# Splitting the mixer and output weights once, ahead of their units, and loading the halves from DRAM

## The chip, the cores and the metric

One core of a Trainium2 chip runs the kernel. The metric is the device time of one execution in microseconds (us); lower is better. TensorE (PE) multiplies, VectorE (DVE), ScalarE (ACT) and GpSimd (POOL) work elementwise, and SyncE (SP) issues every DMA of this kernel, in order, from one queue. Each engine, too, executes its instructions in the order in which they stand.

## The reference

One streaming step of an encoder layer, for 32 + 1024 = 1056 tokens of 1024 features, in float32. Cut to what matters:

```python
x = x + 0.5 * rmsnorm(swiglu(rmsnorm(x), w_gate1, w_up1, w_down1))   # first feed-forward part
h = rmsnorm(x)
p = h @ w_in                              # 1024 x 3072: conv value and gate, and q, k, v, g of 4 heads
c = silu(layernorm(causal_conv31(a * sigmoid(b))))
r = silu(g) * groupnorm(retention(rope(q), rope(k), v))
x = x + rmsnorm(concat(c, r) @ w_out)     # 1024 x 1024
x = x + 0.5 * rmsnorm(swiglu(rmsnorm(x), w_gate2, w_up2, w_down2))   # second feed-forward part
```

The hidden width of a feed-forward part is 2816. The 32 sample tokens carry a state in; all new states are outputs.

## The kernel before

**Splits.** A float32 operand is split into two parts that TensorE multiplies fast: `hi`, a copy rounded to fp32r, and `lo`, the rest, so that a product is hi·hi + hi·lo + lo·hi, three matmuls (L276, L324). For a weight tile `split` (L144) lets ScalarE copy the raw tile to `whi` (L147) and GpSimd, or for some pieces VectorE, subtract to `wlo` (L148). Activations are split by ScalarE and VectorE (L238, L248, L574).

**Units.** The work is a list of units, written out in order by `unit` (L354) and run by `run` (L360). A unit is a block of weights with 512 columns of contraction or less, and one or two visits, each for one half `j` of the tokens (528 of them, as 2 x 264). A visit of a "plain" unit (`visit_plain`, L268) makes four output blocks, 96 matmuls in all where the contraction is 4 x 128; the other kinds, "seven" and "packed", use seven products in place of eight (`visit`, L307). `prep` (L157) is a generator for each unit: it fetches the raw tiles (L155), and then splits them piece by piece. `run` calls it between the products of the unit before (`between`, `plan`), and lets the raw tiles of unit n + 2 be fetched when unit n is done. Raw tiles have 5 buffers, `wh` and `wl` 7 each.

**Order.** The author's code keeps a clock of its own (`now`, advanced by `MM_US` for each matmul) and places work that isn't matmuls at times on it (`later`, `at`); a scheduler then orders each engine's instructions by priority and its own estimate of time. `load` (L113) ties a DMA's place to the matmul that was last written.

**Stages.** First the gate and up units of the first feed-forward part: for each of 11 pairs `fp_` of hidden blocks a gate and an up unit (`up_unit`, L549). The hidden activations are split and spilled to DRAM (`spill`, L567: tiles `hh` and `hl`, tag "g", two buffers; DRAM tensors `hth` and `htl`). Then the down units (L659), in five blocks `DBLK` of 1, 2, 2, 2 and 4 hidden pairs: the spilled tiles come back as `tah`, `tal`, `tbh`, `tbl` (`load_t`, L629), asked for a block ahead by `build` (L642). Norms follow (`post_norm`, `pre_norm`).

The mixer (L701) has 24 plain units: for each half, 4 convolution units (`cu`, L1025) and 4 heads with two units each (`hu`, L1028). Its weights `win` have 12 blocks, each used by both halves, and each time fetched and split anew. VectorE works off the convolution's 31 taps per tile one after the other between other work (`tap`, L757; L760 and L762, 8 tiles). The retention (`retain`, L876) goes in three steps per chunk of tokens: TensorE, ScalarE and VectorE (L884 to L892), then TensorE, VectorE, a power on GpSimd (L927), VectorE (L929), then TensorE and VectorE (L934, L936). The output projection has 8 plain units (L977), from 4 blocks of `wo`, each again fetched and split for either half. The second feed-forward part is as the first.

Of the kernel before, what the change touches and what calls it, by code (L numbers as in the profile page):

```python
# [15 lines left out]
P = 128  # L16
# [39 lines left out]
SPILL_STEP = (1.4, 2.8, 5.6, 9.0)  # L56
POST_STEP = 3.0
NEXT_DELAY = (16.0, 3.0)
MM_US = 0.124
# [6 lines left out]
def layer_kernel(ctx: ExitStack, tc: tile.TileContext, a: dict, o: dict):  # L66
# [90 lines left out]
    def prep(src, nk, kind, dve_lo):  # L157
# [51 lines left out]

        return ws, {"seven": seven, "packed": packed, "plain": plain}[kind]()  # L210

# [148 lines left out]
    def run(opening):  # L360
# [8 lines left out]
        for n, (src, nk, visits, _, kind) in enumerate(program):  # L369
            ws = made[n][0]  # L370
            nxt = made[n + 1][1]
            each = 4 if kind.startswith("plain") else 7
            total = each * len(visits)
            if n + 1 < len(program):
                nkind = program[n + 1][4]
                pieces_ = {"seven": 7, "packed": (7 * program[n + 1][1] + 3) // 4, "plain": 4}[nkind]

                if nkind == kind == "seven":
                    plan = [max(0, total - 8 - (total > 7) * 3)] + [total - 7 + i for i in range(7)]
                else:  # L380
                    plan = [0] + [total - 1 - (pieces_ - 1 - i) * max(1, min(2, (total - 1) // pieces_)) for i in range(pieces_)]
            else:
                plan = []
# [10 lines left out]
            for before, tj, dst, acc, after in visits:  # L394
                if before:
                    before()
                if kind == "plain":
                    visit_plain(ws, tj, nk, dst, after, between, acc)
# [145 lines left out]
    def ffn(xt, wgu, wdn, res, gpost, out, gpre, nxt, lead, first):  # L544
# [4 lines left out]
        def up_unit(fp_, j):  # L549
            def gate_dst():  # L550
                f = hb[fp_, j] = ftile("h")
                return [f[:, i] for i in (0, 3, 1, 2)]
# [106 lines left out]
        for b, (k0, nk) in enumerate(DBLK):  # L659
# [23 lines left out]
            def start(b=b, nk=nk):  # L683
                if b == 0:
                    alloc()
                if b + 1 < len(DBLK):
                    us = 21 * nk * MM_US
# [265 lines left out]
    def out_proj(wt, res, gpost, out, gpre, nxt, also):  # L953
# [23 lines left out]
        for j in (0, 1):  # L977
            for m in range(4):
                unit(a["wo"][m], 4, [o_visit(m, j)], kind="plain")

# [30 lines left out]
    def begin(j):  # L1011
# [4 lines left out]
        for i, b in enumerate(bs):  # L1016
            nrm.add(b, 0.0 if j == 0 else 2.0 * i, sq[i // 2][:, 4 * (i % 2):4 * (i % 2) + 4] if j == 0 else None)
        pre_norm(j, bs, nrm, "f1pre", xt[0], first[0] if j == 0 else None, False, (0.0, 0.0) if j == 0 else (10.0, 3.0),
                 (lambda: later(BEGIN_DELAY, lambda: begin(1))) if j == 0 else lambda: None)

    ffn(xt[0], a["wgu1"], a["wd1"], a["x"], "f1post", x1, "mpre", xt[1], 3, first[0])
    conv, head, free = mixer(xt[1], xt[2])
    win = a["win"]

    def cu(i, j):  # L1025
        unit(win[i], 4, [conv(i, j)], kind="plain")

    def hu(h, j):  # L1028
        for i, v in enumerate(head(h, j)):
            unit(win[4 + 2 * h + i], 4, [v], kind="plain")  # L1030

# [79 lines left out]
```

## Time and profile before

| | us |
|---|---|
| median of 3 runs | 2088.27 (2088.16 to 2093.26) |
| the profiled execution, own time | 2090.26 |
| its span, first to last instruction | 2088.4 |
| TensorE busy | 1931.3 (92%) |
| VectorE busy | 1431.8 (69%) |
| ScalarE busy | 824.4 (39%) |
| GpSimd busy | 1003.0 (48%) |
| mean granted TensorE clock | 0.978 of full speed |

Stages in the profiled execution, by when their instructions begin: gate and up units to 512 us, down units to 783, mixer to 1200, output projection to 1305, then the second feed-forward part.

How to read the profile: every row is of one profiled execution. A group's row has the line of the kernel, the engine and operation, output<-input by the program's names, the shapes, the count; then the busy time, the mean of one in ns, and the idle time of the engine just before, with what ended it. A wait "A <- B" has the total, the number of times, and the longest. `PEclk` is the TensorE clock that was granted, and the DMA share is the mean busy share of the 16 DMA engines. Busy time of TensorE is not TensorE at its peak, so its count in a stretch is set beside it.

### The profile page before, as it was taken

What the parts mean: (1) busy time and instruction counts of PE and PEld (TensorE: products, weight loads), DVE (VectorE), ACT (ScalarE), POOL (GpSimd) and SP (SyncE); (2) the same over time, 40 slices, a digit from 0 to 9 for tenths busy, and PEclk for the clock granted to TensorE, in tenths of its full rate; (3) what the DMA queues carried; (4) which work ended last, traced back from release to release, by engine and by line L of the source; (5) the groups of instructions that cost most, each with busy time, mean ns of one, the idle gap of its engine ahead of it and who ended that gap; (6) DMA issues with size and microseconds to landing.
All of it is one profiled execution on the core that took longest, in us unless ns stands there. A gap on an engine that the chain in (4) does not pass through costs nothing. (4 is left out here: it accounts for less than half of the span.)

```text
span 2088.4 us, 39191 instructions
## 1 busy us (share of the span) xinstructions
PE 1931.3 (92%) x15272; PEld 1889.8 (90%) x15272; DVE 1431.8 (69%) x2386; ACT 824.4 (39%) x1550; POOL 1003.0 (48%) x718
## 2 busy tenths in 40 slices
PE   5988999999999998899889998998999999999995
PEld 4988999999899998888879898987999999989995
DVE  6777666544677368999999846988676644477545
ACT  5444444444322234333343355444444444422221
POOL 3756444454254454455444445456554445344441
PEclk9999999999999999999989999999999999999998
DMA  4354334333965653223422353425344323676742
GB/s 156 98 187 154 129 118 154 132 103 137 351 223 168 216 161 121 62 77 90 125 77 74 106 194 116 148 78 176 115 165 156 129 92 125 240 262 224 254 137 83
DMA packets 143977, 308.60 MB, mean 148 GB/s; under 512 B 17456, under 2 KB 47536, under 8 KB 143792
## 3 DMA queue, kind: packets, MB, share of 16 engines
q1 hardware_dynamic: 143792, 306.10, 44.3%
q8 instruction: 120, 1.97, 0.4%
q14 instruction: 65, 0.53, 0.1%
HBM read 217.54 MB, written 88.50 MB: 147 GB/s over the span
## 5 line engine op out<-in xcount | busy, mean ns | idle before, releaser
L148 POOL TENSOR_TENSOR wlo<-raw,whi 128x512 fp32r<-128x512 f32 x604 | 875.4, 1465 | 847.8 <-ACT whi L147 686.0
L147 ACT ACTIVATE whi<-raw 128x512 fp32r<-128x512 f32 x616 | 363.5, 617 | 647.7 <-issue 172.7
L325 PE MATMUL px<-tbh,whi 128*128 128x264 f32 x832 | 238.6, 287 | 4.3 <-DVE ys L313 2.4
L762 DVE SCALAR_TENSOR_TENSOR cu<-cu,vec 128x558 f32<-128x558 f32 (+1 forms) x240 | 239.6, 1017 | 1.0
L277 PE MATMUL px<-tbh,whi 128*128 128x264 f32 x768 | 226.4, 295 | 11.3 <-ACT cu L727 6.1
L325 PE MATMUL px<-tbh,wlo 128*128 128x264 f32 x832 | 236.6, 284 | 0.0
L325 PE MATMUL px<-tbl,whi 128*128 128x264 f32 x832 | 236.3, 284 | 0.0
L277 PE MATMUL px<-tbl,whi 128*128 128x264 f32 x768 | 223.7, 291 | 0.6 <-DVE tbl L249 0.6
L277 PE MATMUL px<-tbh,wlo 128*128 128x264 f32 x768 | 222.4, 290 | 0.0
L325 PEld LDWEIGHTS px<-tbh,whi 128*128 128x128 f32 x832 | 156.9, 189 | 6.6 <-ACT h L315 2.8
L277 PEld LDWEIGHTS px<-tbh,whi 128*128 128x128 f32 x768 | 149.3, 194 | 12.3 <-ACT cu L727 6.3
L325 PEld LDWEIGHTS px<-tbl,whi 128*128 128x128 f32 x832 | 156.8, 188 | 0.0
L325 PEld LDWEIGHTS px<-tbh,wlo 128*128 128x128 f32 x832 | 156.7, 188 | 0.0
L277 PEld LDWEIGHTS px<-tbl,whi 128*128 128x128 f32 x768 | 148.6, 194 | 1.2 <-DVE tbl L249 0.9
L277 PEld LDWEIGHTS px<-tbh,wlo 128*128 128x128 f32 x768 | 148.5, 193 | 0.2 <-issue 0.2
L318 DVE TENSOR_TENSOR h<-h,px 128x264 f32<-128x264 f32 x152 | 59.0, 424 | 113.3 <-PE px L325 106.1
L325 PE MATMUL px<-tah,whi 128*128 128x264 f32 x416 | 121.0, 291 | 12.0 <-ACT whi L147 8.0
L325 PE MATMUL py<-tbh,whi 128*128 128x264 f32 x416 | 121.7, 293 | 11.0 <-DVE h L318 9.1
L325 PE MATMUL pz<-tbh,whi 128*128 128x264 f32 x416 | 121.5, 292 | 5.2 <-DVE h L318 2.2
L325 PE MATMUL pz<-tah,wlo 128*128 128x264 f32 x416 | 119.6, 287 | 4.9 <-DVE wlo L148 3.1
L325 PE MATMUL py<-tah,whi 128*128 128x264 f32 x416 | 121.1, 291 | 3.2 <-DVE h L601 1.7
L325 PE MATMUL pz<-tbl,whi 128*128 128x264 f32 x416 | 119.4, 287 | 4.5 <-DVE tbl L239 4.5
(218 smaller groups left out, 6030.6 us busy)
## 6 DMA issues: line engine op xcount, KB each, us to landing
raw<-in_wgu SPq DMA_DIRECT2D x224, 256.0 KB, 3.3
hth<-hh SPq DMA_DIRECT2D x28, 924.0 KB, 4.0
htl<-hl SPq DMA_DIRECT2D x28, 924.0 KB, 4.9
raw<-in_win SPq DMA_DIRECT2D x96, 256.0 KB, 3.3
tbh<-hth SPq DMA_DIRECT2D x44, 528.0 KB, 5.8
tbl<-htl SPq DMA_DIRECT2D x44, 528.0 KB, 6.1
raw<-in_wd SPq DMA_DIRECT2D x64, 256.0 KB, 3.0
raw<-in_wd SPq DMA_DIRECT2D x96, 128.0 KB, 3.5
```

The source lines that it names most:

```text
L147: nc.scalar.activation(hi, x[:, :n], AF.Copy)
L148: (nc.vector if dve else nc.gpsimd).tensor_tensor(lo, x[:, :n], hi, ALU.subtract)
L277: mm = nc.tensor.matmul(ps, l[:, w], r, start=k == 0 and i == 0 and n == 0, stop=k == nk - 1 and i == 1 and n == 2)
L318: nc.vector.tensor_tensor(to, to, ps, ALU.add)
L325: mm = nc.tensor.matmul(ps, l[:, w], r, start=start and k == 0 and i == 0, stop=k == nk - 1 and i == 2, skip_group_check=True)
L762: nc.vector.scalar_tensor_tensor(cc, u[:, t:t + m], vec[:, w + t:w + t + 1], cc, ALU.mult, ALU.add)
```

## The change

The 16 weight blocks of mixer and output projection (12 of `win`, 4 of `wo`) are split once, during the first feed-forward part, and kept in DRAM as `hi` and `lo` (tensors `wm`). A block is made in two pairs of its four 128x512 tiles, 32 pairs in all. A pair (`make_pair`) takes one tile of tag "g" (`mk`), loads two raw tiles into one half of it (2 x 256 KB), copies them to the other half on ScalarE (128x1024), subtracts on GpSimd (128x1024), and stores `hi` and `lo` (512 KB each). Eight pairs are placed in the gate and up units, two at each gate unit of the last four `fp_`; the other 24 in the down units, ten of them 12 us apart on the author's clock, then 14 of them 7.5 us apart.

The units of mixer and output projection are of a new kind, "made": `ready_made` loads the four `hi` and four `lo` tiles of a unit straight into `wh` and `wl` buffers (three of each) and two `raw` buffers, and splits nothing. `visit_plain` is unchanged. Their fetches stay where they were: for unit n + 2 when unit n is done.

```diff
+MAKE_STEP = (4.5, 9.0)
...
+        def ready_made():
+            for p in range(4):
+                tags = ("wh", "wl") if p < 3 else ("raw", "raw")
+                pair = []
+                for x, t in zip(src, tags):
+                    w = wp.tile([P, 4 * P], F32R, name=nm("w" + t), tag=t, **({"bufs": 5} if t == "raw" else {}))
+                    load(w.bitcast(F32), x[:, p])
+                    pair.append(w)
+                ws.append(tuple(pair))
+            yield
...
+    def make_later(name, src):
+
+        made_w[name] = hi, lo = [drm.tile([P, 4, 4 * P], F32, name=nm("wm")) for _ in range(2)]
+        to_make.extend((src, hi, lo, q) for q in (0, 1))
+
+    def make_weights(dt):
+        if to_make:
+            later(dt, lambda x=to_make.pop(0): make_pair(*x))
+
+    def make_pair(src, hi, lo, q):
+        n = 4 * P
+        g = flat(fp.tile([P, 8, Q], F32R, name=nm("mk"), tag="g", bufs=2))
+        x, h = g[:, 0:2 * n], g[:, 2 * n:4 * n]
+        for i, b in enumerate(((0, 3), (1, 2))[q]):
+            load(x[:, i * n:(i + 1) * n].bitcast(F32).rearrange("p (k c) -> p k c", k=4), src[:, b])
+
+        def split2():
+            nc.scalar.activation(h, x.bitcast(F32), AF.Copy)
+            nc.gpsimd.tensor_tensor(x, x.bitcast(F32), h, ALU.subtract)
+
+        def store():
+            for to, v in ((hi, h), (lo, x)):
+                nc.sync.dma_start(out=to[:, 2 * q:2 * q + 2], in_=v.bitcast(F32).rearrange("p (a c) -> p a c", a=2))
+
+        later(MAKE_STEP[0], split2)
+        later(MAKE_STEP[1], store)
...
             def gate_dst():
+                if fp_ >= DBLK[-1][0] and j == 0:
+                    for dt in (0.5, 2.5):
+                        make_weights(dt)
...
                 if b == 0:
                     alloc()
+                    for i in range(len(to_make)):
+                        make_weights(12.0 + 12.0 * i if i < 10 else 132.0 + 7.5 * (i - 10))
...
-                unit(a["wo"][m], 4, [o_visit(m, j)], kind="plain")
+                unit(made_w["wo", m], 4, [o_visit(m, j)], kind="made")
...
-        unit(win[i], 4, [conv(i, j)], kind="plain")
+        unit(made_w["win", i], 4, [conv(i, j)], kind="made")
...
-            unit(win[4 + 2 * h + i], 4, [v], kind="plain")
+            unit(made_w["win", 4 + 2 * h + i], 4, [v], kind="made")
```

The new lines move those below: L147 to L148, L148 to L149, L155 to L156, L114 to L115, L927 to L973.

The order of GpSimd in the mixer, second and third convolution tile (`cu`) of the first half and the first head's retention, before; `wlo` are weight halves, `rs` the retention's powers, `tl` the tail of a convolution tile:

```order
L719 MEMSET cu_9809 128x30
L742 COPY tl_10010<-cu_9809 128x30
L927 TENSOR_TENSOR rs_9782<-rs_9782,mhalf 32x1
L927 TENSOR_TENSOR rs_9884<-rs_9884,mhalf 124x1
L148 TENSOR_TENSOR wlo_10210<-raw_10015,whi_10209 128x512
L148 TENSOR_TENSOR wlo_10260<-raw_10220,whi_10259 128x512
L148 TENSOR_TENSOR wlo_10293<-raw_10221,whi_10292 128x512
L148 TENSOR_TENSOR wlo_10331<-raw_10222,whi_10330 128x512
L927 TENSOR_TENSOR rs_9961<-rs_9961,mhalf 124x1
L927 TENSOR_TENSOR rs_10069<-rs_10069,mhalf 124x1
L148 TENSOR_TENSOR wlo_10364<-raw_10223,whi_10363 128x512
L148 TENSOR_TENSOR wlo_10408<-raw_10368,whi_10407 128x512
```

And the same place of GpSimd after the change:

```order
L765 MEMSET cu_10041 128x30
L788 COPY tl_10226<-cu_10041 128x30
L973 TENSOR_TENSOR rs_10010<-rs_10010,mhalf 32x1
L973 TENSOR_TENSOR rs_10112<-rs_10112,mhalf 124x1
L973 TENSOR_TENSOR rs_10185<-rs_10185,mhalf 124x1
L973 TENSOR_TENSOR rs_10293<-rs_10293,mhalf 124x1
L973 TENSOR_TENSOR rs_10367<-rs_10367,mhalf 124x1
L765 MEMSET cu_10584 128x30
```

The splits between the powers are gone, and the powers follow each other.

The order of SP in the second block of the down units, after the change: `raw` from `in_wd` are the block's weights, four tiles to a unit, `tah` to `tbl` spilled tiles, `mk` a make's loads, `wm` its stores:

```order
L156 DMA raw_6440<-in_wd 128x256
L115 DMA mk_6281<-in_win 128x512 x2
L115 DMA tah_6284<-hth_120 128x792
L115 DMA tbh_6286<-hth_120 128x1056
L115 DMA tbl_6287<-htl_121 128x1056
L156 DMA raw_6443<-in_wd 128x256
L115 DMA tah_6461<-hth_120 128x792
L156 DMA raw_6442<-in_wd 128x256
L115 DMA tal_6462<-htl_121 128x792
L156 DMA raw_6441<-in_wd 128x256
L115 DMA mk_6494<-in_win 128x512 x2
L248 DMA wm_96<-mk_6281 128x1024
```

Before, the same place held the weights and spilled tiles alone; now about two loads and two stores of a pair stand among each unit's four weight tiles.

The order of GpSimd at the same place, after the change:

```order
L149 TENSOR_TENSOR wlo_6435<-raw_6347,whi_6434 128x256
L244 TENSOR_TENSOR mk_6281<-mk_6281 128x1024
L149 TENSOR_TENSOR wlo_6527<-raw_6440,whi_6526 128x512
L149 TENSOR_TENSOR wlo_6552<-raw_6441,whi_6551 128x512
L149 TENSOR_TENSOR wlo_6573<-raw_6442,whi_6572 128x512
L149 TENSOR_TENSOR wlo_6592<-raw_6443,whi_6591 128x256
L244 TENSOR_TENSOR mk_6494<-mk_6494 128x1024
```

Here a make's subtraction has come between the last split of one unit and the first of the next; ScalarE's copies stand in the same way.

More of the change, by code (lines that the diff above doesn't have):

```diff
@@ L208, in plain @@
                 yield
-        return ws, {"seven": seven, "packed": packed, "plain": plain}[kind]()
+        def ready_made():
[8 more added lines that the diff above has]
+            yield
+        return ws, {"seven": seven, "packed": packed, "plain": plain, "made": ready_made}[kind]()
+    made_w, to_make = {}, []
+    def make_later(name, src):
[18 more added lines that the diff above has]
+        later(MAKE_STEP[1], store)
     PART = ((0, 0), (1, 0), (0, 1), (1, 1), (0, 2), (1, 3), (1, 2))
@@ L371, in run @@
             nxt = made[n + 1][1]
-            each = 4 if kind.startswith("plain") else 7
+            each = 4 if kind in ("plain", "made") else 7
             total = each * len(visits)
@@ L375, in run @@
                 nkind = program[n + 1][4]
-                pieces_ = {"seven": 7, "packed": (7 * program[n + 1][1] + 3) // 4, "plain": 4}[nkind]
+                pieces_ = {"seven": 7, "packed": (7 * program[n + 1][1] + 3) // 4, "plain": 4, "made": 1}[nkind]
                 if nkind == kind == "seven":
@@ L396, in run @@
                     before()
-                if kind == "plain":
+                if kind in ("plain", "made"):
                     visit_plain(ws, tj, nk, dst, after, between, acc)
@@ L1019, in begin @@
                  (lambda: later(BEGIN_DELAY, lambda: begin(1))) if j == 0 else lambda: None)
+    win = a["win"]
+    for m in range(4):
+        make_later(("wo", m), a["wo"][m])
+    for x in "h0 c0 c1 h1 c2 h2 c3 h3".split():
+        i = int(x[1])
+        for u in (i,) if x[0] == "c" else (4 + 2 * i, 5 + 2 * i):
+            make_later(("win", u), win[u])
     ffn(xt[0], a["wgu1"], a["wd1"], a["x"], "f1post", x1, "mpre", xt[1], 3, first[0])
     conv, head, free = mixer(xt[1], xt[2])
-    win = a["win"]
     def cu(i, j):
-        unit(win[i], 4, [conv(i, j)], kind="plain")
+        unit(made_w["win", i], 4, [conv(i, j)], kind="made")
     def hu(h, j):
         for i, v in enumerate(head(h, j)):
-            unit(win[4 + 2 * h + i], 4, [v], kind="plain")
+            unit(made_w["win", 4 + 2 * h + i], 4, [v], kind="made")
     for j in (0, 1):
```

## The prediction

> **What bounds the kernel now.** I read the page's busy times first, then the busy times by stage, then who waits for whom in the mixer, and last the queue of the DMAs.
>
> ```profile
> PE 1931.3 (92%) x15272; PEld 1889.8 (90%) x15272; DVE 1431.8 (69%) x2386; ACT 824.4 (39%) x1550; POOL 1003.0 (48%) x718
> ```
>
> TensorE is busy 92% of the whole, so the question is where the rest is lost. The stages, with each engine's busy time, its count, then the granted clock, the DMA share and GB/s (the first row is the end of the first feed-forward part's gate and up units, three are its down units, three the mixer, the last the output projection):
>
> ```profile
> core 0: us, PE busy (x) PEld busy (x) DVE busy (x) ACT busy (x) POOL busy (x), PEclk, DMA share, GB/s
> 365.00:512.00 147.00, 146.50 (x1203) 146.08 (x1203) 67.79 (x112) 64.77 (x122) 70.92 (x51) 1.00 0.33 111
> 512.00:574.00 62.00, 58.55 (x449) 55.68 (x448) 39.12 (x90) 23.41 (x55) 19.37 (x16) 1.00 0.97 346
> 574.00:678.00 104.00, 100.95 (x791) 99.60 (x792) 75.90 (x190) 24.71 (x43) 50.77 (x43) 0.97 0.60 195
> 678.00:783.00 105.00, 103.28 (x857) 102.86 (x856) 52.47 (x81) 32.39 (x49) 50.47 (x36) 1.00 0.57 189
> 783.00:835.00 52.00, 45.38 (x359) 44.25 (x358) 42.16 (x53) 25.39 (x44) 23.05 (x17) 0.93 0.40 121
> 835.00:1148.00 313.00, 275.65 (x2107) 265.86 (x2106) 301.29 (x512) 116.59 (x245) 150.87 (x113) 0.95 0.29 85
> 1148.00:1200.00 52.00, 47.42 (x377) 46.66 (x376) 44.13 (x90) 19.30 (x45) 26.73 (x21) 0.97 0.35 103
> 1200.00:1305.00 105.00, 99.70 (x836) 99.07 (x834) 60.85 (x100) 55.66 (x104) 51.83 (x39) 0.99 0.49 155
> ```
>
> The first row is TensorE at full rate: 147.00 us / 1203 = 122 ns a matmul. By that price the mixer's 359 + 2107 + 377 = 2843 matmuls need 347 us, and they take 417: 70 us are lost there, some of it as a clock of 0.93 to 0.97. In the long middle stretch VectorE is busy 301.29 of 313.00 us, 96%. That is the limit there, and TensorE's waits name it:
>
> ```profile
> PE uo L906 <- DVE on L929: 10.7, 7, 6.8
> PE rp L934 <- DVE on L929: 5.9, 4, 3.6
> PE px L277 <- ACT cu L727: 6.1, 1, 6.1
> PE px L277 <- DVE ys L670: 4.8, 1, 4.8
> PE uo L909 <- DMA st<-in_sret: 3.9, 2, 2.3
> ```
>
> VectorE is so full because of GpSimd. Groups from 745 to 1310 us (mixer and output units, with a few splits of the down part), with the count, the busy time and the mean in ns:
>
> ```profile
> L148 POOL TENSOR_TENSOR wlo<-raw,whi 128x512 fp32r<-128x512 f32 x142 | 221.6, 1580 | 144.6 <-ACT whi L147 139.1 <-DMA cu<-in_sconv 2.5 <-PE px L277 1.1
> L147 ACT ACTIVATE whi<-raw 128x512 fp32r<-128x512 f32 x140 | 80.7, 623 | 115.1 <-issue 44.6 <-PE py L277 32.0 <-PE pz L277 31.4
> L762 DVE SCALAR_TENSOR_TENSOR cu<-cu,vec 128x558 f32<-128x558 f32 x120 | 121.7, 1031 | 0.7
> L762 DVE SCALAR_TENSOR_TENSOR cu<-cu,vec 128x528 f32<-128x528 f32 x120 | 118.0, 1002 | 0.3
> ```
>
> VectorE, and below it GpSimd, in order of time (start, length, count at the end):
>
> ```profile
> 900.96 2.91 DVE L762 SCALAR_TENSOR_TENSOR cu<-cu,vec 128x558 f32<-128x558 f32 x4
> 913.22 0.78 DVE L762 SCALAR_TENSOR_TENSOR cu<-cu,vec 128x558 f32<-128x558 f32 x1
> 915.65 2.54 DVE L762 SCALAR_TENSOR_TENSOR cu<-cu,vec 128x558 f32<-128x558 f32 x2
> ```
>
> ```profile
> 902.41 0.12 POOL L719 MEMSET cu<- 128x30 f32 x1 [6.91 <-DMA rd<-hd]
> 912.26 4.62 POOL L148 TENSOR_TENSOR wlo<-raw,whi 128x512 fp32r<-128x512 f32 x2 [1.34 <-ACT whi L147]
> ```
>
> GpSimd stood idle for 6.91 us before 902.41, and there four convolution taps took 2.91 us, 0.73 each. Under the split at 912.26 two took 2.54, 1.27 each. So the splits of the mixer's weights pay twice: their own time on GpSimd, off the path, and the taps' longer time on VectorE, on it.
>
> **The change, part by part.**
>
> *Splits leave the mixer.* Before, 24 units there and 8 of the output projection each split four tiles: 128 copies on ScalarE (623 ns) and 128 subtractions on GpSimd (1580 ns, 202 us). None is left. The 240 taps take 121.7 + 118.0 = 240 us; at 0.73 they take 175, at 0.78 they take 187: VectorE gets 53 to 65 us back, about 52 of them in the middle stretch. What is late next: VectorE then has 301 - 52 = 249 us of work there and TensorE 2107 x 0.122 = 258. Two queues that wait for each other do not both run full; in the stretches before and behind, VectorE is busy 81% (42.16 of 52) and 85%. With 88% in the middle I get 249 / 0.88 = 283 us, 30 less than now. The edges (TensorE needs 44 and 46 us of their 52) I give 2 and 4. Mixer: -36 us. Ends: -12, if the retention's round trips between TensorE and VectorE are what costs and not the load; -60, near TensorE's floor of -70. Output projection: 836 x 0.122 = 102 of 105 us, so -1.
>
> *Direct loads in the mixer.* A unit now loads eight tiles of 256 KB in place of four. That is 1.05 MB more per 11.7 us (96 matmuls), 90 GB/s on top of 85 to 121. The second stretch of the table, at 346 GB/s, shows room for twice that. The loads wait on the SP queue for TensorE to let go of the tiles of the unit before the last one, no longer for GpSimd, which now costs SP this much in the mixer:
>
> ```profile
> SPq L155 <- POOL wlo L148: 234.2, 79, 14.2
> SPq L938 <- DVE hd L936: 20.8, 6, 6.8
> ```
>
> Stores that wait for VectorE (the second row, 3.5 us each) stand in the same queue, ahead of some loads; a load has a unit's time to land, so I take nothing, and up to +10 inside the ends above.
>
> *Makes in the gate and up units.* Eight pairs, each two loads, a copy and a subtraction of 128x1024, and two stores of 512 KB. The copy is about 1.05 us by the row of nearest size, the subtraction about 2.8, twice the row of 512:
>
> ```profile
> L248 ACT ACTIVATE tbh<-ys 128x1056 fp32r<-128x1056 f32 x8 | 8.7, 1085 | 6.2 <-DVE ys L480 6.1
> L148 POOL TENSOR_TENSOR wlo<-raw,whi 128x512 fp32r<-128x512 f32 x77 | 104.7, 1373 | 111.3 <-ACT whi L147 100.8 <-PE py L325 6.4 <-DMA xs<-in_x 3.3
> ```
>
> From 365 to 512 us GpSimd is busy 70.92 of 147, ScalarE 64.77 and the DMA share is 0.33, which hides 23 us, 8 us and 12.6 MB. The pairs use the two buffers of the spills (hh, hl), so a spill can wait for a store. +1, ends 0 and +6.
>
> *Makes in the down units.* 24 pairs. GpSimd gets 67 us more (77 splits take 104.7 of 271 us now) and ScalarE 25; on both, in the new order, a make stands between the last split of one unit and the first of the next, where GpSimd waits for loads today. A make's copy waits for its load, and the next unit's splits stand behind it; but their weights were asked for after that load. A make's store waits for GpSimd's subtraction, and the next weight loads stand behind it on SP; but these wait for splits that stand behind the same subtraction. So the queues add little. By the taps' loss, 0.54 us for each 1.58 us of split, 67 us more of GpSimd would cost VectorE 23 us; but most of its work there reads PSUM, and that is no slower beside a busy GpSimd:
>
> ```profile
> L318 DVE TENSOR_TENSOR ys<-ys,px 128x264 f32<-128x264 f32 x41 | 17.3, 426 | 3.8 <-PE px L325 2.9
> ```
>
> The stage's VectorE time is 167 of 271 us besides, so I take nothing. The Trainium skill ("SBUF — State Buffer", Who interferes with whom) has a rule that speaks for nothing as well: only VectorE operations with two SBUF inputs contend with a GpSimd operation that reads SBUF, and the loser blocks fully. By that rule the two-input operations of the norms at the stage's end would wait up to 2.8 us for each make that they meet; the trace has no make, and I leave it in the ends.
>
> The DMAs are the real price. A pair moves 1.57 MB, all 24 move 37.7 MB; the three down rows moved 346 x 62 + 195 x 104 + 189 x 105 = 61.6 MB. Together 99.3 MB in 271 us, 366 GB/s. What the queue can do (a stretch of 10 us), how long tiles took to land from 505 to 640 us (the last number), and GpSimd's splits for the second block:
>
> ```profile
> 540.00:550.00 10.00, 9.06 (x71) 8.61 (x70) 6.05 (x17) 5.86 (x15) 0.03 (x1) 1.00 1.03 401
> ```
>
> ```profile
> raw<-in_wd SPq DMA_DIRECT2D x40, 128.0 KB, 3.8
> tbl<-htl SPq DMA_DIRECT2D x14, 528.0 KB, 6.7
> ```
>
> ```profile
> 549.97 2.84 POOL L148 TENSOR_TENSOR wlo<-raw,whi 128x512 fp32r<-128x512 f32 x2 [12.23 <-ACT whi L147]
> 562.30 4.86 POOL L148 TENSOR_TENSOR wlo<-raw,whi 128x512 fp32r<-128x512 f32 x4 [6.43 <-ACT whi L147]
> 575.56 4.69 POOL L148 TENSOR_TENSOR wlo<-raw,whi 128x512 fp32r<-128x512 f32 x4 [8.40 <-ACT whi L147]
> ```
>
> Full, it moves 357 GB/s (346 / 0.97) to 401: the stage needs 248 to 278 us of DMA for its 271. The Trainium skill ("DMA: Bandwidth & Descriptors", Specifications) gives about 358 GB/s per core as the limit of the memory; by that the stage would need 277 us and be bound by it, but the row of 401 lies above that limit. While the share is 0.97 a unit's splits begin 12.3 and 13.3 us apart (549.97, 562.30, 575.56), though TensorE needs 84 x 0.122 = 10.3: raw tile, load, additions, split and release follow each other. A pair's 1.57 MB per unit adds 0 to 4.2 us to that cycle, for four units 0 to 17; I take 8. Behind 580 us the share falls to 0.6 and TensorE is busy 97%; I take 2 us each for blocks three and four and for the last block. Down part: +12, ends 0 and +51 (below).
>
> **Sum.** -36 - 1 + 1 + 12 = -24 us. The profiled execution took 2090.26 us (span 2088.4), 2.0 above the median of the runs, 2088.27, so I forecast 2088.3 - 24 = 2064 us.
>
> **The rivals.**
> *The copies' traffic is hidden and VectorE's relief goes through whole*: mixer -52 (the taps at 0.78), output -2, +1, +2: -51, 2037 us. For it: 401 GB/s. Against: TensorE's small waits in the mixer have many releasers.
> *The down part becomes bound by DMA*, and the kernel slower. At 12 us a pair brings 131 GB/s, so from 574 to 678 the share is 0.60 + 0.37 = 0.97, as in the second block: eight units at 12.8 us in place of 10.3, +20. The second block itself gets all 17. In the last block a pair comes every 7.5 us, 210 GB/s: 0.57 + 0.59 = 1.16 of its 105 us, +14 at 401 GB/s or so. +51 in all, against -36: 2088 + 15 = 2103 us. It decides if weight tiles of the down part land in 8 us, not 3.8, behind 580 us, for then the chain has no reserve. Against it: tiles from hth and htl are asked for a block ahead, and pairs can drift into the mixer with its share of 0.29.
> *The splits move and nothing else does*: the mixer's loss is the retention's round trips (TensorE waits for L929, not for taps): -12 there, +12 in the down part: 2088 us.
>
> **Chances.** Forecast 0.64, hidden traffic 0.14, no change 0.10, bound by DMA 0.12. About 0.3%, 6 us, can be told from no change. So faster 0.78, same 0.10, slower 0.12. The range goes from 2036 (the hidden case) to 2090 (mixer at its low end), and leaves out the DMA-bound case and the tails, 2 in 10.
>
> **What would show it.** Right: taps at 0.73 to 0.78 us with both shapes near 770 ns on the mean; VectorE under 90% in the mixer's middle; the mixer some 36 us shorter at a clock nearer 1.00; the DMA share of 574 to 783 us at 0.9 or more, and the down part 5 to 20 us longer, most of it in the second block, with TensorE waiting there for wlo, whi or raw. Wrong: taps still at 1.0 us; a mixer as long as now beside a VectorE that idles; a down part longer by over 35 us, or not at all.

## The result, and the profile after

The changed kernel takes 2068.51 us (median of 5 runs, 2064.78 to 2076.89), the kernel before, on the same chip, 2089.7 (2088.16 to 2093.26): a ratio of 0.99 (95% interval 0.9883 to 0.9917), 21 us less. The forecast was 2064 (2036 to 2090). The sum agrees better than its terms do, so the stages are gone through one by one.

The profiled execution of the changed kernel is the slowest of its five, 2076.89 us, 8.4 above their median; against the 2090.26 of before it is 13.4 us shorter, and that is what its stages can add up to. Busy times and the DMAs' total, from the page of after:

```profile
PE 1929.3 (93%) x15272; PEld 1888.5 (91%) x15272; DVE 1384.3 (67%) x2386; ACT 785.5 (38%) x1454; POOL 892.1 (43%) x622
...
DMA packets 180843, 392.51 MB, mean 189 GB/s; under 512 B 21553, under 2 KB 51633, under 8 KB 180657
```

TensorE has the same 15272 matmuls. GpSimd lost 96 instructions net (128 subtractions gone, 32 of double size come), and the DMAs carry 84 MB more.

Busy times by stage of after (columns as in the prediction's table: busy time and count of each engine, granted clock, DMA share, GB/s). The bounds are, to 1 or 2 us, where the same matmul, counted from the first, begins as at the bounds of before:

```profile
core 0: us, PE busy (x) PEld busy (x) DVE busy (x) ACT busy (x) POOL busy (x), PEclk, DMA share, GB/s
365.00:531.00 166.00, 153.78 (x1207) 151.88 (x1206) 80.33 (x109) 70.17 (x130) 91.51 (x59) 0.97 0.51 173
531.00:597.00 66.00, 60.35 (x450) 57.19 (x448) 41.50 (x98) 26.16 (x58) 25.39 (x19) 0.97 1.00 360
597.00:713.00 116.00, 103.89 (x795) 99.69 (x796) 84.74 (x188) 32.58 (x51) 71.02 (x52) 0.99 0.88 298
713.00:823.00 110.00, 106.27 (x852) 105.45 (x851) 55.75 (x80) 40.20 (x54) 65.13 (x41) 0.97 0.93 328
823.00:874.00 51.00, 44.89 (x361) 43.90 (x360) 40.72 (x55) 20.92 (x33) 15.25 (x8) 0.93 0.92 295
874.00:1141.00 267.00, 260.05 (x2109) 253.96 (x2108) 243.95 (x516) 77.88 (x175) 43.80 (x39) 0.99 0.56 174
1141.00:1187.00 46.00, 46.00 (x383) 45.85 (x383) 32.89 (x78) 10.92 (x30) 5.31 (x6) 1.00 0.67 219
```

The mixer's middle took 267 us in place of 313, at a clock of 0.99 in place of 0.95, with VectorE busy 243.95 of them. Of the 46 us about 30 are TensorE's idle time (37.4 before, 6.9 now) and 16 its matmuls, 260 in place of 276, beside the higher clock; no run separates the clock from the waits. The first row is the surprise: the same 1200 matmuls took 166 us in place of 147. There about 12 us are idle time (0.5 before), and 7 are longer matmuls at a clock of 0.97 in place of 1.00. The convolution's taps, from the groups of VectorE:

```profile
L808 DVE SCALAR_TENSOR_TENSOR cu<-cu,vec 128x558 f32<-128x558 f32 x120 | 92.3, 787 | 0.7
L808 DVE SCALAR_TENSOR_TENSOR cu<-cu,vec 128x528 f32<-128x528 f32 x120 | 89.5, 766 | 0.2
```

They cost 181.8 us in place of 239.7. TensorE's two longest waits from 823 to 1187 us, the mixer, and SP's:

```profile
PE py L318 <- DVE ys L714: 4.8, 1, 4.8
PE uo L952 <- DVE on L975: 2.6, 1, 2.6
```

```profile
SPq L966 <- DVE bs L969: 37.8, 5, 16.3
SPq L115 <- PE py L318: 29.1, 13, 5.2
```

The wait of `uo` for L975 (L929 before) fell from 10.7 to 2.6 us; the one for `ys`, at the mixer's start, is as before. SP's 234 us of waiting for GpSimd are gone; it now waits for VectorE's results to store, and for TensorE to let go of weight tiles.

The next table cuts the traces of before, of after and of the experiments at the same matmuls, and gives each stage's difference from before in us ("gate/up" is the stretch of the last gate and up units that the eight pairs lie in). It is worked out from the start of those matmuls in each trace. One profiled execution stands for each kernel, so 2 or 3 us of one stage are not told apart. "First" is the difference in the earlier gate and up units, where the last kernels have pairs; an empty cell is a stage that the text does not use. The kernels themselves, and what each leaves out, are explained in the next section.

| us, stage against before | gate/up (147) | down 1, 2 (64) | down 3, 4 (102) | down last (105) | mixer (418) | output (108) |
|---|---|---|---|---|---|---|
| after | +18.6 | +2.0 | +13.4 | +5.5 | -54.2 | +0.2 |
| one_block | +6.3 | +0.2 | -1.1 | -0.6 | -63.4 | +0.3 |
| makes_only | +15.5 | +1.7 | +12.6 | +7.1 | +8.6 | +1.3 |
| idle_subtract | +17.3 | -0.3 | +14.8 | +4.6 | -15.7 | +3.5 |
| idle_memset | +14.7 | +1.5 | +14.9 | +5.8 | -48.8 | +0.3 |
| pairs_no_store | +16.3 | +0.8 | +2.8 | +7.7 | -54.3 | |
| pairs_no_split | +14.2 | +2.8 | +6.4 | -0.6 | -54.1 | |
| stores_behind_work | +12.3 | +5.6 | +7.7 | +4.1 | -54.1 | |
| late_copies | +15.5 | +1.5 | +14.3 | +3.9 | -55.4 | |
| late_pairs | +4.3 | +1.7 | +14.6 | +3.7 | -52.7 | +0.1 |
| spread_pairs | +5.4 (first +3.9) | +2.9 | +8.9 | +3.5 | -58.8 | +0.1 |
| win_only | +4.4 (first +6.2) | +1.3 | +2.5 | +0.2 | -53.0 | +1.3 |
| win_fewer_gate | +3.9 (first +0.1) | +2.9 | +8.2 | +2.5 | -58.1 | 0.0 |

### The profile page after: what moved, and what is told of

It reads as the page before. It is cut to its first block, busy times and chain, and to the rows that moved or that the text cites. A ratio compares the mean times of both kernels' runs of the same rounds, so it can differ in the third digit from the quotient of the medians.

```text
span 2075.1 us, 39300 instructions
## 1 busy us (share of the span) xinstructions
PE 1929.3 (93%) x15272; PEld 1888.5 (91%) x15272; DVE 1384.3 (67%) x2386; ACT 785.5 (38%) x1454; POOL 892.1 (43%) x622
## 5 line engine op out<-in xcount | busy, mean ns | idle before, releaser
L149 POOL TENSOR_TENSOR wlo<-raw,whi 128x512 fp32r<-128x512 f32 x476 | 676.1, 1437 | 675.8 <-ACT whi L148 561.1
L148 ACT ACTIVATE whi<-raw 128x512 fp32r<-128x512 f32 x488 | 288.2, 614 | 491.4 <-issue 92.0
L366 PE MATMUL px<-tbh,whi 128*128 128x264 f32 x832 | 240.5, 289 | 4.3 <-DVE ys L354 1.9
L366 PE MATMUL px<-tbl,whi 128*128 128x264 f32 x832 | 237.7, 286 | 0.0
L366 PE MATMUL px<-tbh,wlo 128*128 128x264 f32 x832 | 237.5, 286 | 0.0
L808 DVE SCALAR_TENSOR_TENSOR cu<-cu,vec 128x558 f32<-128x558 f32 (+1 forms) x240 | 181.8, 776 | 0.8
L366 PEld LDWEIGHTS px<-tbh,whi 128*128 128x128 f32 x832 | 158.6, 191 | 6.9 <-ACT h L356 2.5
L366 PEld LDWEIGHTS px<-tbl,whi 128*128 128x128 f32 x832 | 158.5, 190 | 0.0
L366 PEld LDWEIGHTS px<-tbh,wlo 128*128 128x128 f32 x832 | 158.0, 190 | 0.0
L973 POOL TENSOR_TENSOR rs<-rs,mhalf 124x1 f32<-124x1 f32 (+3 forms) x40 | 44.1, 1104 | 219.7 <-DVE rs L972 216.6
L359 DVE TENSOR_TENSOR h<-h,px 128x264 f32<-128x264 f32 x152 | 59.2, 424 | 105.5 <-PE px L366 93.6
L366 PE MATMUL px<-tah,wlo 128*128 128x264 f32 x416 | 120.5, 290 | 1.7 <-POOL wlo L149 1.6
L366 PE MATMUL pz<-tah,whi 128*128 128x264 f32 x416 | 120.4, 289 | 1.5 <-ACT h L356 1.0
L366 PE MATMUL py<-tah,wlo 128*128 128x264 f32 x416 | 120.2, 289 | 1.5 <-POOL wlo L149 1.5
```

Of the source, the lines that this page charges most:

```text
L148: nc.scalar.activation(hi, x[:, :n], AF.Copy)
L149: (nc.vector if dve else nc.gpsimd).tensor_tensor(lo, x[:, :n], hi, ALU.subtract)
L359: nc.vector.tensor_tensor(to, to, ps, ALU.add)
L366: mm = nc.tensor.matmul(ps, l[:, w], r, start=start and k == 0 and i == 0, stop=k == nk - 1 and i == 2, skip_group_check=True)
L808: nc.vector.scalar_tensor_tensor(cc, u[:, t:t + m], vec[:, w + t:w + t + 1], cc, ALU.mult, ALU.add)
L973: nc.gpsimd.tensor_tensor(rs[:L, 1:2], rs[:L, 0:1], mhalf[:L, 0:1], ALU.pow)
```

## The experiments

**The theory at the start.** The mixer gains because no GpSimd subtraction slows VectorE's taps any more; the pairs cost time where they are made. The rivals: the mixer's gain comes from elsewhere (ScalarE's copies, the shorter SP queue), and the direct loads cost something there. All ratios are against the kernel before on the same chip.

**One block made (one_block).** Only the first two pairs are made, and all units load that block's halves, so the mixer has the new loads and the makes are gone.

```diff
+        if made_w:
+            made_w[name] = made_w["wo", 0]
+            return
         made_w[name] = hi, lo = [drm.tile([P, 4, 4 * P], F32, name=nm("wm")) for _ in range(2)]
```

> Only the first weight block is made (2 pairs of 32), and all units of mixer and output projection load that one block's halves, so their results are of wrong weights; the loads keep their number and size. Theory (the mixer gains 54 us because the splits left GpSimd, and the other 30 pairs cost some 40 us of that in the feed-forward part): about 2030 us, with the gate, up and down units as long as before the change, and the mixer at 365 us. Rival A (half of the mixer's gain comes because the pairs shift the order there, not from the missing splits): 2050 us or more. Rival B (the pairs cost little, and the profiled execution was a poor one): 2060 us.

Measured: 2035.03 us, ratio 0.9726 (0.9707 to 0.9745), 57 us less than before; by the two ratios the 30 pairs left out cost the change 36 us (0.0174 x 2090). The direct loads cost the mixer nothing, the down units are back where they were, and the two pairs that stay cost the gate units 6.3 us. The mixer is 9 us shorter than in after. That all units load one block is not the reason by itself: in two kernels below, pairs_no_store and pairs_no_split, they do so too, and their mixers are as after's. About 3 of the 9 lie in the mixer's first 51 us, where after still works off its last pairs (four of their subtractions on GpSimd begin between 822 and 847 us); the rest is open.

**The makes alone (makes_only).** All 32 pairs are made, and nothing uses them; the units of mixer and output projection are plain again.

```diff
-        unit(made_w["win", i], 4, [conv(i, j)], kind="made")
+        unit(win[i], 4, [conv(i, j)], kind="plain")
...
-            unit(made_w["win", 4 + 2 * h + i], 4, [v], kind="made")
+            unit(win[4 + 2 * h + i], 4, [v], kind="plain")
...
-                unit(made_w["wo", m], 4, [o_visit(m, j)], kind="made")
+                unit(a["wo"][m], 4, [o_visit(m, j)], kind="plain")
```

> All 32 pairs are made, but mixer and output projection split their weights themselves as before the change, so nothing reads the made halves. Theory: the cost alone, before plus 30 to 40 us, 2120 to 2130 us; the mixer as long as before, 418 us. Rival A (gain and cost are bound to each other): under 2110 us. Rival B (the pairs cost only the 13 us of the prediction): 2102 us.

Measured: 2137.37 us, ratio 1.0217 (1.0197 to 1.0237), 45 us more. Its stages ahead of the mixer show 37 of them, the mixer 8.6; all of the 8.6 lies in the mixer's first 52 us, where the last four pairs' subtractions stand. The stages ahead agree with those of after, so the price of the makes lies where they are made: in the gate and up units, and in the down units' third and fourth blocks.

**A subtraction put back on GpSimd (idle_subtract).** The new kernel, with one subtraction of 128x512 on an idle tile at each of the 128 output blocks of the made units. The copies, loads and waits of the splits stay gone.

```diff
+            def busy_between():
+                between()
...
+                held(nc.gpsimd.tensor_tensor(pad[0], pad[0], pad[0], ALU.subtract))
```

> The changed kernel, with 128 subtractions of 128x512 put back on GpSimd in mixer and output projection, one at each output block; they read and write a tile that nobody else uses. Theory (the splits cost time because their SBUF reads hold up VectorE's taps): the taps go back to about 1.0 us, and most of the mixer's gain is lost, 2068 + 35 to 50 = 2103 to 2118 us. Rival (the gain comes because TensorE, SP and ScalarE no longer wait for the splits): no more than 8 us slower, 2068 to 2076 us, whatever the taps take.

**Memsets in their place (idle_memset).** Three memsets of that tile at each place, which only write.

```diff
+                for _ in range(3):
+                    held(nc.gpsimd.memset(pad[0], 0.0))
```

> As the run with subtractions, with three memsets of 128x512 in place of each subtraction: GpSimd is busy in the same places but reads nothing. Theory: the taps stay near 0.77 us and the time within 5 us of the changed kernel, 2068 us. Rival (any work of GpSimd delays the powers of the retention that stand behind it, and that is the price): as slow as the run with subtractions, in proportion to GpSimd's busy time.

Measured: 2122.48 us, ratio 1.0143 (1.0115 to 1.017), and 2078.98, ratio 0.9938 (0.9919 to 0.9958). GpSimd's groups of the first and of the second, then VectorE's taps of the first and of the second:

```profile
L441 POOL TENSOR_TENSOR pad<-pad 128x512 f32<-128x512 f32 x128 | 174.8, 1366 | 5.6
```

```profile
L442 POOL MEMSET pad<- 128x512 f32 x384 | 203.4, 530 | 18.6
```

```profile
L816 DVE SCALAR_TENSOR_TENSOR cu<-cu,vec 128x558 f32<-128x558 f32 x120 | 114.2, 966 | 0.7
L816 DVE SCALAR_TENSOR_TENSOR cu<-cu,vec 128x528 f32<-128x528 f32 x120 | 111.2, 941 | 0.4
```

```profile
L817 DVE SCALAR_TENSOR_TENSOR cu<-cu,vec 128x558 f32<-128x558 f32 x120 | 91.9, 784 | 0.5
L817 DVE SCALAR_TENSOR_TENSOR cu<-cu,vec 128x528 f32<-128x528 f32 x120 | 88.6, 756 | 0.5
```

The subtractions take 175 us of GpSimd and slow the taps to 950 ns; the memsets take more of GpSimd, 203 us, and leave the taps at 770. So it is the subtractions, which read, and not GpSimd's being busy that slows the taps (the two also differ in the length of one instruction, 1366 and 530 ns). The Trainium skill ("SBUF — State Buffer", Who interferes with whom) says the same: a VectorE instruction with two SBUF inputs contends with a GpSimd instruction that reads SBUF, not with one that only writes it; both runs agree with it, 950 against 770 ns. The same section of the Trainium skill names VectorE's two-port modes as a second case, which the prediction's "only" leaves out; no run here shows that case. The subtractions alone cost more than the change's net gain of 21 us: by the ratios 51 us (0.0243 x 2090), 38.5 of them in the mixer, where the taps take 43.6 us more of VectorE (225.4 - 181.8). They undo 71% of the mixer's gain, and they take less of GpSimd than the splits did (175 us, not 202). At the same price the 57.9 us that the change took off the taps would be worth 51 of the mixer's 54 us (38.5 / 43.6 x 57.9, an estimate); so little is left for the copies, the loads and SP's waits. The memsets cost 8 us by the ratios, 5 of them in the mixer, and no run says by what.

**The pairs without stores, and without splits (pairs_no_store, pairs_no_split).** Why the makes cost time. Both use the first block's halves for all units, as one_block does. The first leaves out the stores of the other 30 pairs, the second their copies and subtractions.

```diff
-        later(MAKE_STEP[0], split2)
-        later(MAKE_STEP[1], store)
+        if "split" in parts:
+            later(MAKE_STEP[0], split2)
+        if "store" in parts:
+            later(MAKE_STEP[1], store)
```

> As the run with one block made (2035 us), but the other 30 pairs load their tiles, copy and subtract, and leave the stores out; nothing reads them. Theory (the pairs cost time through their stores, which wait on SP ahead of weight loads and bring two thirds of the traffic): 2038 to 2046 us. Rival (the copy on ScalarE waits for its load ahead of TensorE's evictions, and the subtraction holds up GpSimd and VectorE): 2060 us or more, nearly the changed kernel's 2068.

> As the run with one block made (2035 us), but the other 30 pairs load their tiles and store them twice, unsplit: the same DMAs, no work on ScalarE or GpSimd; nothing reads them. Theory (stores and traffic): a store no longer waits for a split, so only the traffic is left, 2045 to 2055 us, most of it in the down units. Rival (copy and subtraction are the cost): 2035 to 2042 us.

Measured: 2065.99 us, ratio 0.9877 (0.9857 to 0.9897), and 2059.04, ratio 0.9836 (0.982 to 0.9852). Neither part alone is the cost; each stage has its own. In the gate and up units both still lose 14 to 16 us; what both keep there, the pairs' loads into the spills' buffers, was not run alone. In the third and fourth blocks of the down units, whose rows follow for the one and the other, what goes with the stores is the larger part of the loss:

```profile
593.00:698.00 105.00, 101.03 (x791) 98.30 (x791) 82.15 (x186) 32.14 (x51) 72.33 (x52) 0.98 0.71 234
```

```profile
593.00:702.00 109.00, 103.64 (x792) 101.07 (x792) 77.10 (x186) 23.43 (x42) 50.22 (x43) 0.96 0.90 318
```

With the DMA share at 0.71 the stage is 2.8 us over before, at 0.90 it is 6.4, at 0.88 and with the splits 13.4. TensorE waits there in after, 12.1 us in all (1.3 before), mostly for evictions by VectorE (L359 and L354, 8.3 us) and for copies of weights; the two longest:

```profile
PE pz L366 <- DVE ys L359: 5.0, 3, 3.2
PE px L366 <- ACT whi L148: 3.1, 3, 1.6
```

Tiles of the down weights land later with it; the medians from issue to landing, in us at the rows' end, of after, of pairs_no_store and of pairs_no_split (2.5 before):

```profile
raw<-in_wd SPq DMA_DIRECT2D x35, 128.0 KB, 5.2
```

```profile
raw<-in_wd SPq DMA_DIRECT2D x35, 128.0 KB, 3.0
```

```profile
raw<-in_wd SPq DMA_DIRECT2D x35, 128.0 KB, 5.2
```

In the last block it is the other way round. Without the splits it loses nothing, at a DMA share of 0.98; without the stores it loses 7.7. Windows of the last block in pairs_no_split, then VectorE's norm in that block in after and in pairs_no_split:

```profile
702.00:807.00 105.00, 103.66 (x862) 103.46 (x861) 51.82 (x82) 31.69 (x45) 43.28 (x31) 1.00 0.98 343
```

```profile
L566 DVE SCALAR_TENSOR_TENSOR ys<-ys,vec,ss 128x528 f32<-128x528 f32 x8 | 10.0, 1322 | 1.3 <-ACT ss L496 1.3
```

```profile
L571 DVE SCALAR_TENSOR_TENSOR ys<-ys,vec,ss 128x528 f32<-128x528 f32 x8 | 6.4, 864 | 1.3 <-ACT ss L501 1.3
```

Beside the makes' subtractions the norm's two-input step takes 1322 ns, without them 864 (865 before), 3.6 us more in all. So a nearly full DMA queue cost nothing there, and the makes' work did. How it reached TensorE is shown in part only: TensorE idles 2 of the 5.5 us that the block lost in after, and its matmuls take 3.6 longer, at a clock of 0.97 where it is 1.00 before and without the splits.

**The stores issued by the engines that fill them (stores_behind_work).** ScalarE issues the store of `hi` right behind its copy, GpSimd that of `lo` behind its subtraction, so that SP doesn't wait for a pair's work.

```diff
-            for to, v in ((hi, h), (lo, x)):
-                nc.sync.dma_start(out=to[:, 2 * q:2 * q + 2], in_=v.bitcast(F32).rearrange("p (a c) -> p a c", a=2))
+            for e, to, v in ((nc.scalar, hi, h), (nc.gpsimd, lo, x)):
+                e.dma_start(out=to[:, 2 * q:2 * q + 2], in_=v.bitcast(F32).rearrange("p (a c) -> p a c", a=2))
```

> The changed kernel, but a pair's store of hi is issued by ScalarE right behind its copy and the store of lo by GpSimd right behind its subtraction, so that no store waits on SP. Theory (SP's wait at a store, ahead of weight loads, is half of the cost or more): 2045 to 2055 us, with the last gate and up units back within 8 us of before. Rival (traffic, or the copies on ScalarE): 2062 us or more.

**Copies and stores later (late_copies).** ScalarE's copy 8.0 us and the stores 12.5 us behind the load in place of 4.5 and 9.0, which was meant to spare ScalarE the wait for a pair's load.

```diff
-MAKE_STEP = (4.5, 9.0)
+MAKE_STEP = (8.0, 12.5)
```

> The changed kernel with a pair's copy and subtraction placed 8 us behind its loads in place of 4.5, and its stores 12.5 us in place of 9. Theory of the stores on SP: no great change, 2062 to 2072 us, or slower, since each pair holds its buffer for longer. Rival (ScalarE waits at the copy for a load that has not landed, ahead of evictions): 2045 to 2055 us, and ScalarE's waits for the pairs' loads gone.

Measured: 2070.78 us, ratio 0.9897 (0.988 to 0.9914), and 2072.65, ratio 0.9908 (0.989 to 0.9925): no gain over the change as it is from either. In the trace of the first, SP's waits for a pair's copy and subtraction (39.1 and 30.9 us in after) are gone, and the time is not shorter: they alone do not set it. Its blocks three and four lost 7.7 us in place of 13.4, but its first two 5.6 in place of 2.0. The second did not do what it was meant to: ScalarE still stands idle for 57.6 us ahead of the pairs' copies (58.3 in after), most of it for their loads, so the rival about ScalarE stays untested.

**The pairs at another time of the gate units (late_pairs).** A new theory was needed for the gate and up units. This is how one wait of TensorE comes about in after, VectorE first, GpSimd below (start, length):

```profile
460.16 0.69 DVE L170 TENSOR_TENSOR s<-raw,raw 128x512 f32<-128x512 f32 x1 [2.71 <-DMA raw<-in_wgu]
460.94 2.71 DVE L171 TENSOR_TENSOR raw<-s,raw 128x512 f32<-128x512 f32 x1
463.58 0.68 DVE L172 TENSOR_TENSOR raw<-raw,raw 128x512 f32<-128x512 f32 x1
464.18 0.42 DVE L359 TENSOR_TENSOR h<-h,py 128x264 f32<-128x264 f32 x1
```

```profile
460.22 2.88 POOL L244 TENSOR_TENSOR mk<-mk 128x1024 fp32r<-128x1024 f32 x1 [1.62 <-ACT mk L243]
```

VectorE waits 2.71 us for a raw tile, and then its addition L171 takes 2.71 us, not 0.69, beside the make's subtraction. Behind the three additions stands the eviction of `py` (L359), and TensorE waits for it:

```profile
PE py L366 <- DVE h L359: 8.2, 6, 1.9
```

So two things met ahead of an eviction: raw tiles that come late, and an addition beside a subtraction of double length. The pairs' loads stand between or right behind the two stores of a spill, and a pair takes a buffer of tag "g" that the spills use. The experiment was to move the pairs into the time in which no spill holds these buffers.

```diff
-                    for dt in (0.5, 2.5):
+                    for dt in (11.0, 13.0):
```

> The changed kernel with one number changed: the two pairs at each of the last four gate units are placed 11.0 and 13.0 us behind the gate unit's start in place of 0.5 and 2.5, so that a pair takes its buffer of tag g after the spills of the pair of hidden blocks before have left theirs, and gives it back before the next spills. All 32 pairs, their loads, copies, subtractions and stores are as before. Theory (the pairs and the spills share two buffers and one queue: a pair's load, or a spill's store behind it, holds up the raw tiles of the gate and up units, so VectorE's additions come late and TensorE waits): the stretch of the last gate and up units comes back from 18.6 us over the kernel before to 2 to 6, and the median from 2068 to about 2055 (2050 to 2060). Rival (the pairs' own work and traffic beside the gate and up units costs it, wherever they stand): the stretch stays 14 to 19 us over, and the median at 2064 to 2072.

Measured: 2063.89 us, ratio 0.9863 (0.9846 to 0.9881), below the interval of the change (0.9883 to 0.9917). Its gate and up units, then L171 in after and in late_pairs (689 ns before, as L170):

```profile
365.00:516.00 151.00, 147.81 (x1201) 146.33 (x1199) 71.50 (x104) 70.08 (x130) 86.69 (x59) 1.00 0.55 188
```

```profile
L171 DVE TENSOR_TENSOR raw<-s,raw 128x512 f32<-128x512 f32 x7 | 8.8, 1263 | 0.3
```

```profile
L171 DVE TENSOR_TENSOR raw<-s,raw 128x512 f32<-128x512 f32 x7 | 4.8, 693 | 0.6
```

TensorE's waits for VectorE's evictions and VectorE's for raw tiles, in that stage of late_pairs (in after 8.2, in the row above, and 16.8):

```profile
PE pz L366 <- DVE h L359: 0.6, 1, 0.6
PE py L366 <- DVE h L359: 0.4, 1, 0.4
DVE s L170 <- DMA raw<-in_wgu: 15.0, 5, 4.8
```

The same pairs with the same traffic (DMA share 0.55) cost 4.3 us, not 18.6: the place of the pairs sets their price there, and the rival (work and traffic) falls. But the cause is not the one that the theory named: the raw tiles hardly come sooner, and VectorE waits for them nearly as long. TensorE waits 3.1 us in all, not 12.2, so the evictions that it needs no longer come late behind that wait. In SP's queue all the pairs' loads now stand behind both stores of a spill (at 412.4 us behind 412.0); in after three of seven stand between them (one at 467.2, between 461.4 and 468.1). Whether that decides, or at what time the additions come, is not shown. The clock is 1.00 again; whether it fell in after because of the waits, no run tells. The median fell by less, 4.6 us, or 8 by the two ratios (0.0037 x 2090), and not by 14; in the median run of the change this stage may have lost less than in the profiled one, which was 8.4 us above it. The slowed addition can be the smaller part of the price at most: in pairs_no_split it takes 684 ns, and the stage still loses 14.2 us, with VectorE waiting 21.5 us for raw tiles and TensorE 9.1 for the evictions behind them.

**More pairs in the gate units (spread_pairs).**

```diff
-                if fp_ >= DBLK[-1][0] and j == 0:
-                    for dt in (0.5, 2.5):
+                if fp_ >= lead and j == 0:
+                    for dt in (11.0, 13.0):
...
-                        make_weights(12.0 + 12.0 * i if i < 10 else 132.0 + 7.5 * (i - 10))
+                        make_weights(12.0 + 14.0 * i)
```

> As the kernel with the pairs late in the gate units, and besides: 16 pairs in place of 8 stand in gate units (two at each of the eight from the fourth on), and the other 16 in the down units, 14 us apart. Theory (a pair that stands clear of the spills costs a gate or up unit little, since the DMAs are a third full there, while in the down units the DMAs are full): the down units give back some 8 to 12 of the 21 us they lost, the gate units cost 2 to 8 in all, and the median is about 2045 (2038 to 2052). Rival (a pair costs some 2 to 3 us wherever it stands): the 16 pairs cost the gate units what the down units give back, and the median is that of the other kernel or above, 2064 to 2076.

Measured: 2060.51 us, ratio 0.9851 (0.983 to 0.9872), not told apart from late_pairs. The down units gave back 4.7 us against late_pairs, the earlier gate units took 4.9 (+3.9 in place of -1.0): the rival was nearer.

**The output projection's blocks not made (win_only, win_fewer_gate).** The output units are plain again and 24 pairs remain: 16 in gate units and 8 in the down units, 22 us apart from 70 us on, in the first (win_only); 8, at the last four gate units, and 16, 14 us apart, in the second (win_fewer_gate). The edit of both against spread_pairs, and then of the first alone and of the second alone:

```diff
-                unit(made_w["wo", m], 4, [o_visit(m, j)], kind="made")
+                unit(a["wo"][m], 4, [o_visit(m, j)], kind="plain")
...
-    for m in range(4):
-        make_later(("wo", m), a["wo"][m])
```

```diff
-                        make_weights(12.0 + 14.0 * i)
+                        make_weights(70.0 + 22.0 * i)
```

```diff
-                if fp_ >= lead and j == 0:
+                if fp_ >= DBLK[-1][0] and j == 0:
```

> As the kernel with 16 pairs spread over eight gate units, but the output projection's four blocks are not made: its 8 units are plain again and split their own weights. The other 24 pairs are kept: 16 in gate units, and 8 in the down units, from 70 us after their start and 22 us apart, behind the block in which the DMAs are full. Theory (the output projection gains nothing from its made weights, and each pair in the down units costs through its traffic): the output projection stays within 3 us, the down units come back to 2 to 8 us over the kernel before (15 with 16 pairs), and the median is 2045 to 2056. Rival (the splits of the output units' weights cost there, beside the mixer's end, what their 8 pairs cost in the down units): the mixer's last stretch and the output projection get 5 to 10 us longer together, and the median stays at 2058 to 2064.

> As the kernel with the output units plain again (24 pairs), but with 8 pairs in place of 16 in gate units, those of the last four, and 16 in the down units, 14 us apart from 12 us on. Theory (a pair in a gate unit, clear of the spills, costs about half a microsecond, one in the down units about 1 us): the earlier gate units are as in the kernel before (within 1 us), the down units 12 to 17 us over it, and the median is 2052 to 2062, 4 to 10 above that with 16 pairs in gate units. Rival (a pair costs the same wherever it stands): the median is within 3 us of that with 16 pairs in gate units.

Measured: 2058.24 us, ratio 0.9833 (0.9818 to 0.9849), and 2051.45, ratio 0.9805 (0.9791 to 0.982). The second is the fastest that makes all it needs, 41 us less than before and about 20 less than the change. It was expected above the first, and came out 7 below. The output projection is as long with plain units as with made ones (+1.3 and 0.0 against +0.2); the mixer's last stretch, where their splits begin, is up to 2 us longer (46.2 and 46.9 us against 44.9 in after). So its pairs brought 3 us at most, and without them the down units are 6.4 us shorter than in late_pairs (13.6 against 20.0). The eight pairs in the last gate units cost about 4 us, the eight in the earlier ones 6; the 8 in the down units cost 4.0, the 16 there 13.6. So a pair costs half a microsecond to one wherever it stands clear, and the rule that the gate units are the cheaper place fell. The middles of the mixer differ as well, win_only's first:

```profile
848.00:1117.00 269.00, 260.76 (x2107) 255.31 (x2106) 250.53 (x525) 75.22 (x173) 41.18 (x40) 0.97 0.54 169
```

```profile
851.00:1114.00 263.00, 259.15 (x2108) 253.64 (x2107) 244.45 (x515) 77.61 (x175) 39.00 (x39) 0.99 0.57 177
```

Six of the 7 us lie there, at a clock of 0.97 against 0.99, in two programs with the same mixer; why the clock differs is open.

## Why the prediction was right, and which of its steps failed

**The mixer, -36 us.** The mechanism was right and the size too small: -54.2. The taps came out as said, 776 ns on the mean and 57.9 us less of VectorE (53 to 65), and idle_subtract and idle_memset show that GpSimd's subtractions are the cause. What was mis-sized is the step from VectorE's relief to the stage: "VectorE 88% busy" of 249 us of work gave 283 us for the middle, and it took 267. VectorE's work there is 244, 5 less, and it is busy 91% of the time; TensorE takes 126.7 ns a matmul (267 / 2107) where the prediction's full rate is 122. Both run nearer to full than the neighbouring rows had suggested. The edges gave 8 us in place of 6. The sign for it, VectorE under 90%, was missed by one per cent.

**The output projection, -1 us.** +0.2 in place of -1; win_fewer_gate (0.0) shows that it needs no made weights.

**The makes in the gate and up units, +1 us with ends 0 and +6.** This step failed: +18.6 in the profiled run, 12.3 to 17.3 in seven other kernels with pairs at that place. It counted busy shares (GpSimd 48%, DMAs at 0.33) and took what fits into them as hidden. The wait for shared buffers was named and given 6 us at most. What was not seen is that VectorE's additions stand ahead of evictions in its queue: where they wait for raw tiles, or run beside a subtraction of double length, TensorE waits too (8.2 of its 12.2 us there). That the granted clock falls to 0.97 in such a stage, 7 us more, was not in the sum either, and its cause is open. late_pairs shows what the step would have been worth with the pairs elsewhere, +4.3.

**The makes in the down units, +12 us.** 20.9 in sum, and not where the step had put it. The second block was to lose 8; it and the first lost 2.0 together, with a DMA share of 1.00. Blocks three and four, given 4 together, lost 13.4, and the last, given 2, lost 5.5. The step let the pairs' traffic be moved where the pairs were placed. But in the first two blocks, whose DMAs were nearly full before (0.97), only 2.3 MB more were moved (360 x 66 against 346 x 62), about one and a half pairs. The blocks three and four moved 14.3 MB more, at a share of 0.88 in place of 0.60; there tiles of 128 KB land in 5.2 us, not 2.5, and TensorE waits for evictions and copies. The last pairs came as late as the mixer's start. In the last block a step that the prediction had left in the "ends" was seen: the norm's two-input steps, slowed beside the makes.

**The rivals.** Hidden traffic (2037): the mixer's half of it came true, -54 against -52, but the makes' price did not vanish. Bound by DMA (2103): its blocks three and four got two thirds of their 20 us; it overstated the second block (+17) and the last (+14, where a share of 0.98 without splits cost nothing). No change (2088): the mixer fell with the taps, and rose with them in idle_subtract, so the retention's round trips were not what cost most.

**Why the forecast held all the same.** By the profiled execution of after the terms are -54, 0, +19 and +21, -14 in sum, beside -36, -1, +1 and +12. The gain and the price were both put too low, by 17 and 27 us, and the median lies 8 below the profiled run. That the forecast came within 5 us is luck: the errors took each other away.

## What to carry to other kernels

Price work that is moved under other work by where it stands in each queue and whose buffers it takes, not by the idle share of the engine; here the same eight pairs cost 18.6 or 4.3 us by their place. Before weights are prepared ahead, ask of each stage that uses them whether it was held up at all: the mixer was, the output projection was not, and 8 of 32 pairs cost more than they brought. Where GpSimd works beside VectorE, look at whether both read SBUF: beside a subtraction of 2.88 us a VectorE addition of 0.69 us took 2.71.

## What the runs showed of the hardware that had not been expected

A memset on GpSimd, 128x512 in 530 ns, leaves VectorE's taps at 770 ns, though GpSimd is busy for 203 us with them. A single GpSimd subtraction of 2.88 us held a VectorE addition, begun 0.72 us after it, until about its own end (2.71 us in place of 0.69), where the prediction had read off taps of 1.27 us in place of 0.73. And a DMA share of 0.98 at 343 GB/s cost the down units' last block no time (105 us, as before); TensorE's one wait there was for VectorE:

```profile
PE pz L323 <- DVE ys L719: 1.3, 1, 1.3
```

So a high DMA share did not by itself say what a stage loses: in the third and fourth blocks 0.88 went with a loss of 13.4 us with all the makes' work, and 0.90 without their splits with 6.4.
